# The sum of the state-space group's small products in the pool of the coefficients instead of that of the activations' parts

## The chip, the cores and the metric

The kernel runs on one core of a Trainium2 chip. The metric is the device time of one execution in microseconds (us), as the median of several runs. A profiled execution is one more run, from which the trace comes.

The core's engines work side by side and each takes its instructions in a fixed order: TensorE (PE) multiplies, VectorE (DVE), ScalarE (ACT) and GpSimd (POOL) work on elements, and SyncE (SP) issues the transfers from and to memory. An instruction that has to wait holds up all that stands behind it on its engine. On SP it is a transfer's issue that waits, and what stands behind it is the next transfers.

## The reference

Two layers, each of three sublayers. In between lies the mixing sublayer, one group of which is a diagonal complex state-space model (S5).

```python
h = layer_norm(ALPHA*h + 0.5*swiglu(h, ffn1_in[l], ffn1_out[l]), ...)    # "f1"
h = layer_norm(ALPHA*h + concat(pool, nsa, s5)(h @ w_in) @ w_out, ...)   # "mix"
h = layer_norm(ALPHA*h + 0.5*swiglu(h, ffn2_in[l], ffn2_out[l]), ...)    # "f2"

def swiglu(x, w_in, w_out):
    gate, up = split(x @ w_in, 2);  return (silu(gate) * up) @ w_out

def s5_mixer(u, ...):        # 16 groups, 64 complex states each
    ar, ai = exp(lr*dt) * (cos(li*dt), sin(li*dt))
    bbr, bbi = (fr, fi) * (b_re, b_im)               # complex product
    h = associative_scan(h[t] = a*h[t-1] + bb @ u[t])
    y = Re(c @ h) + d_skip*u;   ...
```

Sizes: 512 tokens, width 1024, 2816 hidden columns in the feed-forward parts, all in fp32.

## The kernel before

**Products.** Every fp32 operand of a large product is split into two parts, a rounded one (`hi`, made by ACT) and the rest (`lo`, made by DVE), and the product is three matmuls: hi·hi, hi·lo, lo·hi. Weights come in units of 128x1024. SP loads a unit into one of three buffers `st` (line 97), ACT and DVE split it (lines 131 and 132) into a slot of `ring`, or into the pair `wh`/`wl`, six places in all. A place comes free when PE has used the unit that lies there, and an `st` buffer when the unit in it has been split.

**The first feed-forward part of a layer, `ffn` with kind f1.** The hidden columns come in 22 tiles of 128. Tiles 0 to 3 and 18 to 21 are made by `pair` (lines 343 to 345 on PE, two PSUM banks `g` and `u`, then ACT's silu at line 547 and DVE's product at line 548), the rest by `quad`. Then `project` multiplies by the output weights: for each tile k, 24 matmuls (line 491) into eight PSUM banks `o`, which are all the banks there are. Before tile k its activations are split into `ap`k by `split` (lines 602 and 603), one tile ahead. The eight banks `o` rotate with all other PSUM tiles: a bank is taken over once its last reader is done.

**The state-space matrices, `s5_matrices`.** It is a generator that `ffn` steps: one step before the pairs 18 to 21, six after pair 20, and one at each of the first tiles of `project` (`STEPS_AT`, `GB_AT`). POOL computes the complex products (`cmul`, lines 759 to 764): the matrices `ebr`, `ebi`, the coefficients `fcr`, `fci`, `nfci` in the tile `s5cf`, the matrices `gr`, `gi`, and by doubling the tables `tabc`, `tabs` with the scratch tile `dbl`. PE makes sixteen small products of these into the bank `kk` (lines 796 and 798), DVE adds the input's `dm` and writes the sum to `s5kk` (line 803), and eight small transfers carry blocks of `s5kk` to their places in `tm` (line 816).

**Two pools.** `pp` ("parts") has four buffers of 4 KB in each partition, used in turn by whoever asks next: `s5raw`, `s5d`, `s5ebr`, `s5ebi`, `s5kk`, and after these the parts `ap0`, `ap1`, ... Whoever takes a buffer waits until all readers of its last holder are done. The second pool ("s5t", `ap2` in `s5_matrices`) has two buffers, for `s5cf` and `dbl`. When `s5_matrices` is through, that pool is closed, and the memory goes to `ln_g` and `ln_b`, the norm's scale and shift, whose loads (lines 424 and 425) therefore wait for the end of all work on the tiles of "s5t".

The program's order on each engine is worked out when the kernel is built, before it runs; an instruction's place in it depends on when its buffers and inputs were reckoned to be free.

Of the kernel before, what the change touches and what calls it, by code (L numbers as in the profile page):

```python
# [216 lines left out]
class Trunk:  # L217
# [526 lines left out]
    def s5_matrices(self, l, ap, ap2):  # L744
# [10 lines left out]
        def slot(name, pool=ap):  # L755
            return pool.tile([128, 8, 128], F32, tag="u", name=name)
# [37 lines left out]
        for j in range(8):  # L794
# [4 lines left out]
                             start=False, stop=True)  # L799
            if j % 2 and j < 7:  # L800
                yield
        kks = slot("s5kk").rearrange("p a b -> p (a b)")[:, :256]
        ve.tensor_tensor(kks, kk[:, :256], dm, op=ALU.add)
        yield
        for src, dst in ((ebr, self.er), (ebi, self.ei)):
# [870 lines left out]
```

## Time and profile before

| | |
|---|---|
| Median of 3 runs | 1946.25 us (1940.8, 1946.25, 1946.46) |
| Profiled execution, its own time | 1939.41 us |
| Its span, first to last instruction | 1937.6 us |
| Mean granted clock of TensorE | 0.987 of full speed |
| PE busy | 1875.5 us (97%) |
| DVE busy | 1365.1 us (70%) |
| ACT busy | 811.3 us (42%) |
| POOL busy | 528.1 us (27%) |

The time of the profiled execution is 1.81 us above its span; the median of the three runs lies 6.84 us above the profiled execution. PE is busy nearly all the time, so a stretch in which it is not is looked up by itself, with what ended it.

### The profile page before, as it was taken

To read this page: it belongs to the slowest core of one execution; us is meant where nothing else is said; L and a number is where in the kernel's file an instruction comes from. 1 tells how busy PE (TensorE), PEld (TensorE's weight loads), DVE (VectorE), ACT (ScalarE), POOL (GpSimd) and SP (SyncE) were. 2 spreads that over 40 slices of the span, in tenths; PEclk is the share of its full clock that TensorE was granted. 3 is DMA by queue.
4 is the path that set the end of the run, shared out by engine and by line. 5 is a ranking of instruction groups with operands and counts; after the bars stand their busy time and mean duration, and the time that the engine had idled before them with its cause. 6 is when DMAs were issued, how large, how long until landed. Compare 5 with 4: busy or idle time off the path is not lost.

```text
span 1937.6 us, 30490 instructions
## 1 busy us (share of the span) xinstructions
PE 1875.5 (97%) x12164; PEld 1672.8 (86%) x12164; DVE 1365.1 (70%) x1926; ACT 811.3 (42%) x1388; POOL 528.1 (27%) x539
## 2 busy tenths in 40 slices
PE   9999959999999999999999999699999999999998
PEld 7999848888788999998899997588887889999886
DVE  8998324667986889874598982246679768989634
ACT  5454213234772354543235442231457714455430
POOL 3332920104331433300043329101043313322001
PEclk9999979999999999999999999799999999999999
DMA  7233233222103132343203341341221122232421
GB/s 249 92 120 122 85 101 125 69 69 88 45 20 102 65 109 100 119 163 126 81 30 102 110 146 54 112 142 42 80 77 45 42 90 66 99 112 96 157 94 44
DMA packets 57214, 183.59 MB, mean 95 GB/s; under 512 B 11248, under 2 KB 12016, under 8 KB 57072
## 3 DMA queue, kind: packets, MB, share of 16 engines
q1 hardware_dynamic: 57072, 181.64, 28.3%
q8 instruction: 96, 1.57, 0.3%
q14 instruction: 46, 0.38, 0.1%
HBM read 179.19 MB, written 2.10 MB: 94 GB/s over the span
## 4 chain that ended last, share of the span: by engine, by line
PE 82%; POOL 7%; DVE 7%; DMA 2%; issue 1%; ACT 1%; SPq 1%; DVEq 0%; ACTq 0%; POOLq 0%
PE o L491 28%; PE qb L345 3%; PE qb L344 3%; PE qb L343 3%; PE qa L345 3%; PE qa L344 3%; PE qa L343 3%; PE qc L345 3%; PE qc L344 3%; PE qc L343 3%; PE o L1314 2%; PE pt L1298 2%; PE qd L345 2%; PE qd L344 1%; PE qd L343 1%; DVE ring L132 1%
## 5 line engine op out<-in xcount | busy, mean ns | idle before, releaser
L132 DVE TENSOR_TENSOR ring<-st,ring 128x1024 fp32r<-128x1024 f32 (+1 forms) x257 | 354.3, 1387 | 251.0 <-ACT ring L131 248.5
L131 ACT ACTIVATE ring<-st 128x1024 fp32r<-128x1024 f32 (+1 forms) x257 | 270.3, 1054 | 374.1 <-PE o L491 170.8
L491 PE MATMUL o<-ring,ap 128*128 128x512 f32 x1440 | 332.5, 392 | 43.9 <-DVE a L548 43.9
L491 PEld LDWEIGHTS o<-ring,ap 128*128 128x128 f32 x1440 | 272.3, 189 | 101.6 <-DVE a L548 44.7
L383 POOL TENSOR_TENSOR mv<-mv,expo 128x1 f32<-128x1 f32 x24 | 35.6, 1481 | 629.4 <-DVE mv L382 629.4
L182 POOL TENSOR_TENSOR st<-st,sb 128x512 f32<-128x512 f32 x64 | 95.5, 1493 | 186.4 <-DVE ring L132 114.3
L343 PE MATMUL qb<-th,ring 128*128 128x256 f32 x512 | 143.4, 280 | 0.4 <-DVE u L707 0.4
L343 PE MATMUL qa<-xh,ring 128*128 128x256 f32 x512 | 143.4, 280 | 0.0
L345 PE MATMUL qa<-xh,ring 128*128 128x256 f32 x512 | 143.4, 280 | 0.0
L344 PE MATMUL qa<-xl,ring 128*128 128x256 f32 x512 | 143.4, 280 | 0.0
L344 PE MATMUL qb<-tl,ring 128*128 128x256 f32 x512 | 143.4, 280 | 0.0
L345 PE MATMUL qb<-th,ring 128*128 128x256 f32 x512 | 143.4, 280 | 0.0
L491 PE MATMUL o<-wh,ap 128*128 128x512 f32 x448 | 125.5, 391 | 0.0
L177 POOL TENSOR_TENSOR sumg<-sb 128x512 f32<-128x512 f32 x32 | 57.4, 1792 | 177.8 <-DMA sb<-in_ffn_in 177.8
L132 DVE TENSOR_TENSOR wl<-st,wh 128x1024 fp32r<-128x1024 f32 x51 | 62.2, 1228 | 56.3 <-ACT wh L131 56.0
L491 PEld LDWEIGHTS o<-wh,ap 128*128 128x128 f32 x448 | 83.5, 188 | 17.6 <-DVE vw L717 0.6
L344 PEld LDWEIGHTS qa<-xl,ring 128*128 128x128 f32 x512 | 97.6, 191 | 0.1
L344 PEld LDWEIGHTS qb<-tl,ring 128*128 128x128 f32 x512 | 97.6, 191 | 0.0
L343 PEld LDWEIGHTS qb<-th,ring 128*128 128x128 f32 x512 | 96.4, 188 | 0.5 <-issue 0.5
L343 PEld LDWEIGHTS qa<-xh,ring 128*128 128x128 f32 x512 | 96.3, 188 | 0.2
L345 PEld LDWEIGHTS qa<-xh,ring 128*128 128x128 f32 x512 | 96.1, 188 | 0.0
L345 PEld LDWEIGHTS qb<-th,ring 128*128 128x128 f32 x512 | 96.1, 188 | 0.0
(459 smaller groups left out, 5159.5 us busy)
## 6 DMA issues: line engine op xcount, KB each, us to landing
st<-in_ffn_in SPq DMA_DIRECT2D x110, 512.0 KB, 3.3
st<-in_ffn_out SPq DMA_DIRECT2D x88, 512.0 KB, 3.3
sb<-in_ffn_in SPq DMA_DIRECT2D x64, 512.0 KB, 3.3
st<-in_w_out SPq DMA_DIRECT2D x16, 512.0 KB, 3.8
st<-in_w_b SPq DMA_DIRECT2D x8, 512.0 KB, 4.4
st<-in_w_a SPq DMA_DIRECT2D x8, 512.0 KB, 4.6
ln_g<-in_ln_g SPq DMA_DIRECT2D x6, 512.0 KB, 4.1
ln_b<-in_ln_b SPq DMA_DIRECT2D x6, 512.0 KB, 5.5
```

Of the source, the lines that this page charges most:

```text
L131: self.nc.scalar.activation(hi, t, AF.Copy)
L132: self.nc.vector.tensor_tensor(lo, t, hi.bitcast(F32), op=ALU.subtract)
L177: po.tensor_tensor(s[:, f], b[:, f], b[:, r], op=ALU.add)
L182: po.tensor_tensor(a[:, f], a[:, f], b[:, f], op=ALU.subtract)
L343: mm(out, lhsT=ah, rhs=bh, start=start, stop=False, skip_group_check=skip)
L344: mm(out, lhsT=ah, rhs=bl, start=False, stop=False, skip_group_check=skip)
L345: mm(out, lhsT=al, rhs=bh, start=False, stop=stop, skip_group_check=skip)
L383: nc.gpsimd.tensor_tensor(mv[:, 2:3], mv[:, 2:3], self.expo, op=ALU.pow)
L491: mm(ps[t][f], lhsT=a[:, q], rhs=w[:, 512 * f:512 * f + 512], start=(k == first and a is ah and w is wh), stop=end)
L1298: nc.tensor.transpose(ps[:, 128 * k:128 * k + 128], p[:, i, 128 * k:128 * k + 128], ident)
L1314: mm(o[64 * i:64 * i + 64], lhsT=self.v[:, b, k, 64 * g:64 * g + 64], rhs=pt[:, i, 128 * k:128 * k + 128], start=False, stop=b == 1 and k ...
```

## The change

The tile `s5kk` is taken from the pool "s5t" instead of "parts". One call differs:

```diff
@@ -799,7 +799,7 @@ def s5_matrices(self, l, ap, ap2)
                              start=False, stop=True)
             if j % 2 and j < 7:
                 yield
-        kks = slot("s5kk").rearrange("p a b -> p (a b)")[:, :256]
+        kks = slot("s5kk", ap2).rearrange("p a b -> p (a b)")[:, :256]
         ve.tensor_tensor(kks, kk[:, :256], dm, op=ALU.add)
         yield
```

No instruction is added, none is taken away, and none has another size. What changes is who takes which buffer after whom. In "parts", `ap0` now takes the buffer of `s5raw` (before: of `s5d`), `ap1` that of `s5d` (of `s5ebr`), `ap2` that of `s5ebr` (of `s5ebi`), `ap3` that of `s5ebi` (of `s5kk`), and `ap4` follows `ap0` (before `ap0` too, from its other place). In "s5t", `s5cf` has the first buffer as before, `s5kk` has the second, and `dbl` takes the first after `s5cf` (before: the second, which was empty). The order on PE is the same; on the other engines it moves at the following places, here in layer 0, and at the same ones in layer 1.

ACT, where the product with the output weights begins: `ei` is the last copy of the state-space matrices, `ap_2462`, `ap_2465`, `ap_2523` and `ap_2599` are `ap0` to `ap3`, `wh_2492` is unit 4 of the output weights and `ring<-st_2418` unit 5, and `a_2340<-g_2390` is the silu of tile 21.

```order
 L810 ACTIVATE ei<-et_2380 128x512
-L602 ACTIVATE ap_2462<-a_242 128x512
 L602 ACTIVATE ap_2465<-a_242 128x512
 L602 ACTIVATE ap_2523<-a_396 128x512
+L602 ACTIVATE ap_2599<-a_396 128x512
 L131 ACTIVATE wh_2492<-st_2338 128x1024
 L547 ACTIVATE a_2340<-g_2390 128x512
-L602 ACTIVATE ap_2599<-a_396 128x512
 L131 ACTIVATE ring<-st_2418 128x1024
```

The split of `ap3` moves ahead of unit 4 and of the silu; on DVE its second half moves in the same way, from a place ahead of the product of tile 21 (line 548) to one behind the halves of `ap1` and `ap2`.

ACT, some 13 instructions earlier: `a_2217<-g_2159` is the silu of tile 18, `wh_2246` and `ring<-st_2187` are the two weight units of tile 21, and `ring<-st_2215` is unit 0 of the output weights.

```order
 L547 ACTIVATE a_2217<-g_2159 128x512
 L131 ACTIVATE wh_2246<-st_2088 128x1024
+L602 ACTIVATE ap_2462<-a_242 128x512
 L131 ACTIVATE ring<-st_2187 128x1024
 L131 ACTIVATE ring<-st_2215 128x1024
```

The split of `ap0` has come here; it takes the buffer of `s5raw`, so it waits for POOL's last product that reads `s5raw`.

SP, the transfers around the norm's loads: `st_2418`, `st_2446`, `st_2496` and `st_2552` are the units 5, 6, 7 and 8 of the output weights. First where `ln_g` stood, then where it stands.

```order
 L97 DMA st_2418<-in_ffn_out 128x1024
-L424 DMA ln_g<-in_ln_g 128x1024
-L816 DMA tm<-s5kk 16x8x16
-L816 DMA tm<-s5kk 32x8x16
-L816 DMA tm<-s5kk 48x8x16
-L816 DMA tm<-s5kk 64x8x16
 L97 DMA st_2446<-in_ffn_out 128x1024
```

```order
+L816 DMA tm<-s5kk 64x8x16
+L424 DMA ln_g<-in_ln_g 128x1024
 L97 DMA st_2496<-in_ffn_out 128x1024
+L425 DMA ln_b<-in_ln_b 128x1024
 L97 DMA st_2552<-in_ffn_out 128x1024
```

Before, `ln_g` stood ahead of all eight transfers to `tm` and of unit 6; now it stands behind them, and ahead of unit 7.

POOL, the end of `gr` and `gi` and the beginning of the doubling.

```order
+L763 TENSOR_TENSOR s5cf<-s5cf,prm_a4r 128x256
+L764 TENSOR_TENSOR gi<-gi,s5cf 128x16x16
+L822 TENSOR_SCALAR gi<-gi 128x1024
+L760 TENSOR_TENSOR dbl<-tabs 128x8
+L761 TENSOR_TENSOR tabc<-tabc,dbl 128x8
+L763 TENSOR_TENSOR dbl<-tabs,tabc 128x8
+L759 TENSOR_TENSOR tabc<-tabc 128x8x2
```

Before, the instructions of the first four doublings stood between those of `fcr`, `gr` and `gi`; now all that write `dbl` stand behind the last of `gi`.

## Rows read from the trace of the kernel before

**Rows 1.** The page: the chain that ended last, by engine.

```profile
PE 82%; POOL 7%; DVE 7%; DMA 2%; issue 1%; ACT 1%; SPq 1%; DVEq 0%; ACTq 0%; POOLq 0%
```

**Rows 2.** Waits from 236 to 268 us: who waited for whom, total, times, longest.

```profile
ACT ap L602 <- DMA tm<-s5kk: 28.3, 1, 28.3
...
PE o L491 <- DVE a L548: 22.0, 1, 22.0
```

**Rows 3.** Timeline of PE, both layers: start, length, line, operands, count [idle before].

```profile
227.13 1.52 PE L809 MATMUL et<-cst,s5ebi 128*128 128x128 f32 x8
...
239.41 4.47 PE L491 MATMUL o<-ring,ap 128*128 128x512 f32 x19
...
265.83 19.27 PE L491 MATMUL o<-ring,ap 128*128 128x512 f32 x77 [21.95 <-DVE a L548]
284.94 0.62 PE L491 MATMUL o<-wh,ap 128*128 128x512 f32 x2
...
1202.14 4.47 PE L491 MATMUL o<-ring,ap 128*128 128x512 f32 x19
...
1247.57 0.62 PE L491 MATMUL o<-wh,ap 128*128 128x512 f32 x2
```

**Rows 4.** Stretches: width, busy PE, PEld, DVE, ACT, POOL, granted clock, DMA, GB/s.

```profile
266.00:268.00 2.00, 2.00 (x5) 1.61 (x6) 0.91 (x1) 0.00 (x0) 0.00 (x0) 0.50 0.66 229
268.00:270.00 2.00, 2.00 (x8) 1.53 (x8) 0.49 (x1) 1.58 (x2) 0.00 (x0) 0.73 0.71 248
```

**Rows 5.** The chain in order of time, two links: start, length.

```profile
254.16 1.27 POOL tabs L764
...
265.18 0.61 DVE a L548
```

**Rows 6.** SP: the issue of `ln_g` and the next, and its longest wait.

```profile
255.45 0.33 SPq L424 DMA_DIRECT2D ln_g<-in_ln_g  x1
255.83 2.75 SPq L816 DMA_DIRECT2D tm<-s5kk  x4
...
SPq L424 <- POOL tabs L764: 29.8, 1, 29.8
```

**Rows 7.** Timeline of POOL, layer 0, and its last doubling in layer 1.

```profile
206.64 1.60 POOL L762 TENSOR_TENSOR s5cf<-s5raw,prm_fi 128x256 f32<-128x256 f32 x1
...
214.60 0.61 POOL L763 TENSOR_TENSOR s5cf<-s5raw,prm_fr 128x256 f32<-128x256 f32 x1
...
230.72 1.06 POOL L763 TENSOR_TENSOR s5cf<-s5cf,prm_a3r 128x256 f32<-128x256 f32 x1
...
1217.15 1.26 POOL L764 TENSOR_TENSOR tabs<-tabs,dbl 128x512 f32<-128x512 f32 x1
```

**Rows 8.** Timeline of DVE: two beside POOL's products, two in a step of `project`.

```profile
206.36 1.41 DVE L132 TENSOR_TENSOR ring<-st,ring 128x1024 fp32r<-128x1024 f32 x1 [3.97 <-ACT ring L131]
...
229.87 2.46 DVE L603 TENSOR_TENSOR ap<-a,ap 128x512 fp32r<-128x512 f32 x3 [3.77 <-ACT ap L602]
...
275.35 1.23 DVE L132 TENSOR_TENSOR ring<-st,ring 128x1024 fp32r<-128x1024 f32 x1 [4.01 <-ACT ring L131]
276.50 0.69 DVE L603 TENSOR_TENSOR ap<-aq,ap 128x512 fp32r<-128x512 f32 x1
```

**Rows 9.** Timeline of ACT: unit 7 and `ap5`, then unit 8, in `project`.

```profile
274.26 1.06 ACT L131 ACTIVATE ring<-st 128x1024 fp32r<-128x1024 f32 x1 [4.26 <-PE o L491]
275.23 0.61 ACT L602 ACTIVATE ap<-aq 128x512 fp32r<-128x512 f32 x1
279.70 1.06 ACT L131 ACTIVATE ring<-st 128x1024 fp32r<-128x1024 f32 x1 [3.86 <-PE o L491]
```

**Rows 10.** Transfers of a unit, us to landing: 258 to 259.2, 262.6 to 263, all.

```profile
st<-in_ffn_out SPq DMA_DIRECT2D x1, 512.0 KB, 4.4
...
st<-in_ffn_out SPq DMA_DIRECT2D x1, 512.0 KB, 5.4
...
st<-in_ffn_out SPq DMA_DIRECT2D x88, 512.0 KB, 3.3
```

## The prediction

> **What bounds the kernel now.** I read the page first, then the waits of a stretch, then the timelines of each engine in it. The chain that ended last runs over PE for 82% of the span, so time is to be had only where PE stands still or where the chain leaves it. It leaves it for POOL for 7% of 1937.6 us, some 135 us [rows 1]. In the chain in order of time this is two runs of the state-space matrices, one in each layer, of which the first ends at 255.43 us with the last doubling and then, through SP, a transfer to `tm` and ACT, comes to DVE's line 548 and so back to PE [rows 5]. The list of waits tells the same from the other end: ACT waits 28.3 us ahead of a split (line 602) for the transfer to `tm`, and PE 22.0 us for line 548 [rows 2].
>
> With the order of the program the links can be named. SP's queue holds `ln_g` ahead of the eight small transfers to `tm`. `ln_g` waits 29.8 us, until the last doubling is done, since it takes over the memory of the coefficients' pool [rows 6]. The transfers to `tm` are held up behind it, though their input was ready long before. `ap3` takes the buffer of `s5kk`, which these transfers read, so ACT stands at `ap3` until they have landed. On DVE the product of tile 21 (line 548) is queued behind `ap3`'s second half; it reads the last PSUM bank that `project` needs, so PE stops after 19 of the 24 matmuls of tile 0 [rows 3].
>
> **What a stop costs.** A step of `project` is 5.44 us (279.70 less 274.26 [rows 9]). Undisturbed, tile 4, the first with weights in `wh`, would begin 4 x 5.44 = 21.76 us after tile 0: at 261.17 and 1223.90 us. It begins at 284.94 and 1247.57 [rows 3]. That is 23.77 and 23.67 us late, 47.44 together. Of each, 21.95 us is the idle stretch; the rest fits the granted clock afterwards, 0.50 (1.2 GHz) from 266 to 268 us and 0.73 in the mean up to 270 [rows 4]: (1 - 0.50) x 2 + (1 - 0.73) x 2 = 1.5 us, and 0.1 before 266.
>
> **What the change does to this.** No instruction comes or goes, so nothing is paid for work. `ap3` takes the buffer of `s5ebi`, free once PE has transposed it at about 228.7 us [rows 3], and stands before the silu of tile 21 on ACT. The wait for `tm` is gone, and with it the 47.44 us. Three waits are new or moved.
>
> *First, ap0 waits for `s5raw`* and stands on ACT early, in the pairs of tiles 18 to 21. POOL's last product that reads `s5raw` ended at 215.21 us [rows 7]. ACT will stand there until then, and behind it are two weight splits (1.0 us each), the silu of tile 19 (as long as `ap`'s first half, 0.6 [rows 9]) and more; DVE stands too, at `ap0`'s second half. The first that PE misses is the bank which the silu of tile 19 empties: the last of the four groups of transposes takes it, half way through the row at 227.13, near 227.9 us [rows 3]. So `ap0` may start as late as 227.9 - 0.6 - 2.0 - 0.6 = 224.7 us. It has 9.5 us to spare, more if POOL is quicker while DVE stands. The weights behind it are wanted later still, at the second half of tile 21. I cost this at nothing; from below because a split that PE doesn't yet want can give nothing, from above by those 9.5 us.
>
> *Second, the doublings* of 1 to 8 columns now run in a row behind `gi` rather than among other products. POOL's work stays the same, but its end may move. Two things move it. (a) POOL is slowed beside DVE: the product at 206.64 took 1.60 us beside DVE's weight split, against 0.61 for one of the same size at 214.60, and one beside `ap`'s second halves took 1.06 [rows 7, 8]. So a weight split costs POOL 1.0 us and a second half of `ap` 0.45. Until 256 us DVE will now do, beyond what it did before, the splits of units 5 and 6 and the second halves of `ap3` and `ap4`: 2 x 1.0 + 2 x 0.45 = 2.9 us. (b) Each of some 24 doubling products now waits for the one before it, where they were interleaved. I take 0.04 us each, 1.0 us; between 0 and 0.13 each the bounds are 0 and 3 us. In all 3.9 us, between 0 and 5.9.
>
> For (a) there is a rule too. The Trainium skill, page "SBUF — State Buffer", section "Who interferes with whom", says that a VectorE `tensor_tensor` with two inputs in SBUF contends with a GpSimd instruction that reads SBUF, and that the one that comes later is blocked for the whole instruction. By that rule, with DVE's lengths of 1.23 and 0.69 us [rows 8], (a) would be 2 x 1.23 + 2 x 0.69 = 3.8 us rather than 2.9. The trace agrees in kind: 0.99 us were added beside a split of 1.41.
>
> *Third, `ln_g` still waits for the doublings,* and unit 7 of the output weights is now queued behind it on SP; on ACT the split of unit 7 stands ahead of that of `ap5` [rows 9], so PE's tile 5 hangs on it. Counted from the start of `project`: the last doubling ended after 16.0 us in layer 0 (255.43 - 239.41) and 16.3 us in layer 1 [rows 3, 5, 7]; with 3.9 more after 20.1. `ln_g` is issued, and 0.4 us later [rows 6] unit 7. A unit lands after 3.3 us as a rule, after 4.4 behind `ln_g` and some of `tm`, after 5.4 behind `ln_b` [rows 10]. I take 4.4, the row behind `ln_g`: unit 7 is there after 24.9 us. Tile 5 begins after 5 x 5.44 = 27.2 us, and wants `ap5`'s first half then, which is ready 0.97 + 0.61 = 1.6 us after unit 7; and the second half 4 matmuls or 0.9 us later, which is ready 2.9 us after unit 7 (277.19 less 274.26 [rows 8, 9]). So unit 7 must be there after 25.2 us. It is, by 0.3 us. With both upper bounds (16.3 + 5.9 + 0.4 + 5.4 = 28.0) PE would wait 2.8 us in each layer, with the lower ones not at all. Since 0.3 us is less than what I don't know, I take 0.5 us in each layer. In the kernel before the same queue cost nothing, because PE stood still anyway.
>
> The rest of SP's queue is no danger: the transfers to `tm` no longer stand behind `ln_g`, so they go out as soon as `s5kk` is written, up to the 29.8 us of that wait [rows 6] earlier.
>
> **The sum.** 47.4 - 2 x 0.5 = 46.4 us less. Against the profiled execution's own time, 1939.41: 1893.0 us. The median of the three runs lies 6.84 us above it; two of three runs were there, one and the profiled one were not, so I add half, 3.4, and predict **1896 us** (2.6% below the median of before). What is gained in `project` isn't given back: behind it PE is the chain again.
>
> **Rivals.**
> *A. A new stop at tile 5.* The mechanism of the third point, with a doubling run or a landing beyond my bounds. For it: the margin is 0.3 us, and DVE, so far at rest during POOL's last 16 us, now works. Against it: ACT and DVE stand at unit 7 by then, so DVE stops slowing POOL. If unit 7 lands 5 us late, 10 us of 47 are lost, and the time is 1896 + 9 = 1905 us. By the page's rule alone unit 7 lands 0.9 us later, 0.6 past its limit, which is inside what I took.
> *B. Slower: ACT's wait at `ap0`.* Its place is the first point. It costs from 224.7 us on, one for one, and decides the sign from 224.7 + 23.7 = 248.4 us: POOL would have to leave `s5raw` 33 us later than it did. At 40 us later in each layer, the time is 1946 + 2 x 7 = 1960 us. Nothing in the trace holds POOL that long; its wait for the load of `s5raw` stands before all this and isn't touched.
> *C. No change:* the stop has a second cause that ends at the same moment, as units not loaded or a bank not free. Against it: the wait's only releaser is `tm` [rows 2], and what ACT had behind `ap3` ran at once. The time would be 1946 us.
>
> **Chances.** The forecast 0.80, A 0.13, B 0.04, C 0.03. A measurement of this kernel can tell about 0.3% from no change, 5.8 us, which is also the spread of the three runs. Faster is the forecast and A, 0.93; same 0.03, slower 0.04. The range: at its lower end no new stop and a median as low as the profiled execution, 1892, less 2 for the runs' spread; at its upper end the stop of 2.8 us in each layer, 1892.0 + 5.6, and the whole 6.8: 1904, and 2 for the lesser half of A. So 1890 to 1906.
>
> **What would show it.** Right: no row of PE waiting for line 548 near 244 us in either layer; tile 4 some 21.8 us after tile 0; POOL's part of the chain near nothing; ACT waiting at line 602 for POOL up to about 215 us; the last doubling near 259 us and unit 7 landed near 264. Wrong: a wait of PE ahead of tile 5, near 266.6 us, with ACT behind unit 7's transfer, by more than 3 us (A); PE waiting near 228 us for a bank (B); the same stop with another releaser (C).

## The result and the profile after

The changed kernel takes 1898.17 us (median of 4 runs, 1896.81 to 1901.27), the kernel before 1946.36 us on the same chip (4 runs, 1940.8 to 1949.62). The ratio is 0.9758, with a 95% interval of 0.9732 to 0.9783: 48.2 us less by the medians. The forecast was 1896 us, within 1890 to 1906. The profiled execution of the changed kernel took 1899.04 us, with a span of 1897.1 us and a mean granted clock of 0.997; before these were 1939.41, 1937.6 and 0.987. One execution, the profiled one of e8 below, took 3090.99 us at a mean granted clock of 0.556 and stays out of every comparison.

The page of the changed kernel: busy time by engine, PE and its granted clock in 40 slices, and the chain that ended last.

```profile
PE 1875.3 (99%) x12164; PEld 1672.4 (88%) x12164; DVE 1372.8 (72%) x1926; ACT 810.6 (43%) x1388; POOL 527.4 (28%) x539
...
PE   9999999999999999999999999999999999999998
...
PEclk9999999999999999999999999999999999999999
...
PE 81%; POOL 8%; DVE 7%; DMA 2%; issue 1%; ACT 1%; SPq 0%; DVEq 0%; ACTq 0%; POOLq 0%
```

PE's busy time is what it was, 1875.3 us against 1875.5; the span shrank by 40.5 us, so what went is idle time. But POOL still has 8% of the chain, after 7% before [rows 1]. This is the first sign that something new stops PE behind POOL. The timeline of PE shows it, in `project` of layer 0 and then of layer 1.

```profile
240.16 21.92 PE L491 MATMUL o<-ring,ap 128*128 128x512 f32 x96
261.92 0.61 PE L491 MATMUL o<-wh,ap 128*128 128x512 f32 x2
...
269.69 29.33 PE L491 MATMUL o<-ring,ap 128*128 128x512 f32 x120 [2.17 <-ACT ap L602]
...
1183.36 21.92 PE L491 MATMUL o<-ring,ap 128*128 128x512 f32 x96
...
1211.83 1.19 PE L491 MATMUL o<-ring,ap 128*128 128x512 f32 x4 [1.10 <-ACT ap L602]
1213.17 26.59 PE L491 MATMUL o<-ring,ap 128*128 128x512 f32 x116 [0.15 <-DVE ap L603]
```

The first four tiles run through, 96 matmuls in a row, where before 19 were followed by a stop of 21.95 us [rows 3]. Tile 4 begins 21.76 us after tile 0 in both layers (1205.12 less 1183.36 in the second). Ahead of tile 5 there is a new, short stop: 2.17 us in layer 0, 1.10 and 0.15 in layer 1. The chain in order of time says what it hangs on.

```profile
260.64 1.30 POOL tabs L764
262.37 5.59 DMA st<-in_ffn_out
268.06 1.06 ACT ring L131
269.69 1.30 PE o L491 x4
```

POOL's last doubling ends, unit 7 is transferred, ACT splits it and then `ap5`, and PE goes on. SP's queue shows why a doubling holds up a weight unit.

```profile
228.17 5.39 SPq L816 DMA_DIRECT2D tm<-s5kk  x8
261.96 0.35 SPq L424 DMA_DIRECT2D ln_g<-in_ln_g  x1
262.37 0.42 SPq L97 DMA_DIRECT2D st<-in_ffn_out  x1
262.83 0.42 SPq L425 DMA_DIRECT2D ln_b<-in_ln_b  x1
```

All eight transfers to `tm` are issued from 228.17 us on, where the first began at 255.83 before [rows 6]. `ln_g` waits for the end of the doublings as it did, and unit 7 is now the transfer behind it. In the waits of all engines from 190 to 280 us (total, times, longest) this and the moved split `ap0` appear as follows.

```profile
ACT ring L131 <- DMA st<-in_ffn_out: 24.7, 3, 20.6
...
ACT ap L602 <- POOL s5cf L763: 14.5, 1, 14.5
...
PE o L491 <- ACT ap L602: 2.2, 1, 2.2
```

ACT's wait for `tm` and PE's 22.0 us for line 548 [rows 2] are gone. ACT stands 14.5 us at `ap0` and 20.6 us at unit 7; PE feels nothing of the first, and 2.2 us of the second.

### The profile page after: what moved, and what is told of

The parts are those of the page before. It is cut to its first block, busy times and chain, and to the rows that moved or that the text cites. A ratio compares the mean times of both kernels' runs of the same rounds, so it can differ in the third digit from the quotient of the medians.

```text
span 1897.1 us, 30481 instructions
## 1 busy us (share of the span) xinstructions
PE 1875.3 (99%) x12164; PEld 1672.4 (88%) x12164; DVE 1372.8 (72%) x1926; ACT 810.6 (43%) x1388; POOL 527.4 (28%) x539
## 4 chain that ended last, share of the span: by engine, by line
PE 81%; POOL 8%; DVE 7%; DMA 2%; issue 1%; ACT 1%; SPq 0%; DVEq 0%; ACTq 0%; POOLq 0%
PE o L491 26%; PE qb L345 3%; PE qb L343 3%; PE qb L344 3%; PE qa L345 3%; PE qa L343 3%; PE qa L344 3%; PE qc L345 3%; PE qc L343 3%; PE qc L344 3%; PE o L1314 2%; PE pt L1298 2%; PE qd L345 2%; PE qd L343 2%; PE qd L344 2%; DVE ring L132 1%
## 5 line engine op out<-in xcount | busy, mean ns | idle before, releaser
L132 DVE TENSOR_TENSOR ring<-st,ring 128x1024 fp32r<-128x1024 f32 (+1 forms) x257 | 358.3, 1402 | 255.3 <-ACT ring L131 252.9
L177 POOL TENSOR_TENSOR sumg<-sb 128x512 f32<-128x512 f32 x32 | 51.0, 1595 | 178.0 <-DMA sb<-in_ffn_in 178.0
L491 PEld LDWEIGHTS o<-wh,ap 128*128 128x128 f32 x448 | 83.5, 188 | 17.6 <-DVE vw L717 0.6
```

Of the source, the lines that this page charges most:

```text
L132: self.nc.vector.tensor_tensor(lo, t, hi.bitcast(F32), op=ALU.subtract)
L177: po.tensor_tensor(s[:, f], b[:, f], b[:, r], op=ALU.add)
L491: mm(ps[t][f], lhsT=a[:, q], rhs=w[:, 512 * f:512 * f + 512], start=(k == first and a is ah and w is wh), stop=end)
```

## The experiments

Two theories say what the 47 us before hung on. **Q**, the queue: `ln_g`, waiting on SP for the doublings, stands ahead of the transfers to `tm`; whatever puts it behind them takes the stop away. **B**, the buffers: `ap3` takes over `s5kk`, so the cure is that `ap3` gets another buffer. The change does both at once. What is left after it, the stop at tile 5, was to be traced to the same queue, and the two parts of POOL's longer run, (a) DVE beside it and (b) the doublings in one row, to be told apart.

### e1: the changed kernel again

No edit; it is the measure for e2 to e4, with which it shared a chip.

> The changed kernel itself once more, as the thing that the other runs of this series stand beside on the same chip. 1898 us, within 3 us; PE stops ahead of tile 5 of the output product for 2.2 us in layer 0 and 1.3 us in layer 1.

1900.38 us (4 runs), before 1943.87 us (9 runs), ratio 0.9772 [0.9757, 0.9788]. The timeline of PE in this kernel, tile 5 in layers 0 and 1:

```profile
268.18 27.93 PE L491 MATMUL o<-ring,ap 128*128 128x512 f32 x120 [2.19 <-ACT ap L602]
...
1209.85 29.08 PE L491 MATMUL o<-ring,ap 128*128 128x512 f32 x120 [2.50 <-ACT ap L602]
```

The new stop is there again, 2.19 and 2.50 us, so it is no accident of one execution. Its length changes from one to the next, though, and in a third trace of the same program (e7 below) layer 1 has no stop at all.

### e2: the old buffers, with the norm's loads held back

The kernel before, in which `ln_g` and `ln_b` are each first written by a one-column copy that needs `ap12`. Their loads then come late in the program, and on SP behind `tm` and the units. `ap3` still takes the buffer of `s5kk`.

```diff
-                self.load_gb(*(gp.tile([128, D], F32, name=n) for n in ("ln_g", "ln_b")), l, ln_i)
+                ts = [gp.tile([128, D], F32, name=n) for n in ("ln_g", "ln_b")]
+                if f1:
+                    for t in ts:
+                        nc.scalar.activation(t[:, :1], parts[GB_AT][0][:, :1].bitcast(F32), AF.Copy)
+                self.load_gb(*ts, l, ln_i)
```

> The kernel before, with s5kk left in the pool of the parts, but with the loads of the norm's scale and shift made to depend on ap12, by a copy of one column (two ACT instructions in each layer), so that they stand late in SP's queue, behind unit 16 of the output weights. Theory Q (the gain came from SP's queue: what held ap3 was that the small transfers stood behind ln_g): the whole 47.4 us are gone, and the stop at tile 5 isn't there either, so 1895 us, 3 below the changed kernel. Theory B (the gain came from the buffers: ap3 has to give up the buffer of s5kk, since its transfers land late in any case): PE still stops after 19 matmuls, and the time stays within 10 us of 1946.

1893.91 us (4 runs), ratio 0.9739 [0.9724, 0.9755]. The timeline of PE in `project` of layer 0:

```profile
239.53 21.92 PE L491 MATMUL o<-ring,ap 128*128 128x512 f32 x96
...
266.73 27.36 PE L491 MATMUL o<-ring,ap 128*128 128x512 f32 x120
```

and of SP's queue:

```profile
227.54 5.40 SPq L820 DMA_DIRECT2D tm<-s5kk  x8
...
290.59 0.33 SPq L424 DMA_DIRECT2D ln_g<-in_ln_g  x1
```

Neither stop is there. With `ln_g` out of the way the transfers to `tm` go out from 227.54 us on, and `ap3` has its buffer in time although it is still that of `s5kk`, in the kernel as built. The buffer does no harm by itself: what Q says of this run holds, and what B says of it (a stop after 19 matmuls, a time near 1946 us) does not. The page of this kernel shows how little of the chain POOL still has:

```profile
PE 90%; DVE 7%; issue 1%; DMA 1%; ACT 1%; POOL 1%; SPq 0%; DVEq 0%; ACTq 0%
```

POOL is down to 1% of the chain, which I had expected of the change itself.

### e3: the changed kernel, with the norm's loads held back

The same edit in the changed kernel.

> The changed kernel with the same late loads of scale and shift. If the stop at tile 5 (2.2 and 1.3 us) comes from unit 7 standing behind ln_g, it goes, and the time is 3.4 us below the changed kernel of this series, 1895 us. If it came from ACT or DVE being late after their wait at ap0, it stays, and the time is that of the changed kernel. Beside the kernel before with late loads it tells what the move of s5kk is worth once the queue is right: nothing, within 2 us, by theory Q; some 45 us by theory B.

1893.21 us (5 runs), ratio 0.9735 [0.9721, 0.9749]. Its timeline of PE has no stop, and in the waits from 195 to 300 us `ap0` stands:

```profile
ACT ap L606 <- POOL s5cf L767: 14.7, 1, 14.7
```

Two things follow. First, e3 and e2 are equal (0.7 us apart, within what the runs of one kernel scatter): once the queue is in order, it is worth nothing that `s5kk` lies in the other pool. ACT's early wait of 14.7 us at `ap0`, which e3 has and e2 has not (its other buffers keep it away), costs nothing either, as the prediction's first point said. Second, e3 is 7.2 us faster than e1. In e1's trace the two stops sum to 4.69 us, and the 120 matmuls behind them took 0.57 and 1.72 us longer than the 27.36 us of e2: 7.0 us. So the rest of what `ln_g` costs in the changed kernel is accounted for by the stop ahead of tile 5 and the matmuls just behind it, as closely as runs that scatter by 4 us can tell.

### e4: a tile of its own for the sum

The changed kernel, with `s5kk` in a pool of its own (1 KB in each partition). It takes nobody's buffer, and nobody takes its own while it matters. `dbl` then has an empty buffer, as before the change, the doublings stand among the other products again, and `ln_g` again ahead of `tm` and of unit 6.

```diff
-                steps = self.s5_matrices(l, pp, right(gbc, "s5t", 2))
+                t2 = right(gbc, "s5t", 2)
+                self.kks = right(gbc, "s5k", 1).tile([128, 256], F32, name="s5kk")
+                steps = self.s5_matrices(l, pp, t2)
...
-        kks = slot("s5kk", ap2).rearrange("p a b -> p (a b)")[:, :256]
+        kks = self.kks
```

> s5kk in a tile of 1 KB of its own, in neither pool, so that ap3 takes the buffer of s5ebi as in the changed kernel, but the doubling can start early as in the kernel before, and ln_g is again put ahead of the small transfers and of unit 6 in SP's queue. Theory Q: the old stop is gone since ap3 hangs on no transfer, but unit 6 now lands some 27 us after the start of the output product (last doubling at 19, four small transfers 3, landing 4.4 to 5.4), and ap4, behind it on ACT, is wanted at 21.8: a new stop of about 7 us ahead of tile 4 in each layer and a slow clock behind it, 1905 to 1912 us. Theory B: the buffers are right, so it is as fast as the changed kernel or 3 us faster, 1895 to 1898.

1907.18 us (4 runs), ratio 0.981 [0.9796, 0.9825]: 6.8 us slower than e1. The timeline of PE:

```profile
270.20 1.04 PE L491 MATMUL o<-wh,ap 128*128 128x512 f32 x2 [4.79 <-ACT ap L604]
...
1215.94 1.22 PE L491 MATMUL o<-wh,ap 128*128 128x512 f32 x2 [5.09 <-ACT ap L604]
```

and of SP's queue in layer 0:

```profile
261.06 0.33 SPq L424 DMA_DIRECT2D ln_g<-in_ln_g  x1
261.44 2.76 SPq L818 DMA_DIRECT2D tm<-s5kk  x4
264.30 0.57 SPq L97 DMA_DIRECT2D st<-in_ffn_out  x1
```

No buffer is short, the old stop is gone, and yet PE stops 4.8 and 5.1 us, one tile earlier than in e1: unit 6 stands behind `ln_g` and four transfers to `tm`. That is Q again, by another route. Which unit stands behind `ln_g` sets which tile waits. The time is in the range that I gave for Q; the stops are shorter than the 7 us that I expected, since unit 6 landed some 25 us after the start of `project` and not 27. With the matmuls of tile 4 behind them, which took 7.2 and 7.1 us instead of 5.44, the stops make 13.3 us, and e4 is 14.0 us slower than e3, which has none.

The run says something of B as well. `ln_g` stands ahead of the transfers to `tm` here as it did before the change, and a buffer other than that of `s5kk` for `ap3` is enough to take the old stop away: 36.7 us less than the kernel before. The old stop thus needed both, the place of `ln_g` and `ap3`'s buffer. B is wrong in that the buffer is not needed for the gain (e2) and does not bring all of it (e4), where the place of `ln_g` does.

### e5: the last doubling twice

The changed kernel, with the last doubling done twice, to see whether a longer run of POOL goes into the stop one for one.

```diff
+            for _ in range(1 + (2 * n == NCH)):
                 cmul(tc[:, :, hi], ts[:, :, hi], tc[:, :, lo], ts[:, :, lo], cn, sn, tmp[:, :, :n])
```

> The changed kernel with the last doubling of the tables done twice (same values), six products of POOL more, 6.9 us in each layer. In SP's order ln_g now stands behind unit 7 and ahead of unit 8. If the stop is set by the end of the doubling through SP's queue, it moves to tile 6 and grows: last doubling some 28.5 us after the start of the output product, unit 8 landed at 35, wanted at 6 x 5.44 + 0.9 - 2.9 = 30.6, so some 4.5 to 5.5 us in each layer instead of 2.2 and 1.3, and the time is 6 to 9 us over the changed kernel, 1904 to 1907 us. If the stop has nothing to do with POOL's end, it stays at tile 5 with its length, or is gone, and the time is 1895 to 1898.

1908.47 us (4 runs, 1905.3 to 1911.74), before 1942.29 us (13 runs), ratio 0.9827 [0.981, 0.9843]. The timeline of PE in layers 0 and 1:

```profile
279.45 24.06 PE L491 MATMUL o<-ring,ap 128*128 128x512 f32 x96 [3.29 <-ACT ap L602]
...
1226.38 23.59 PE L491 MATMUL o<-ring,ap 128*128 128x512 f32 x96 [6.58 <-ACT ap L602]
```

In layer 0 the stop is 3.29 us. In both it has moved on by one tile: 96 matmuls are left behind it up to the next tile with weights in `wh`, not 120, so it stands ahead of tile 6. The longer run is paid for: 9.9 us of stops, against 3.4 in the changed kernel's own trace, where I expected 9 to 11. They are not alike in the two layers because POOL's run began 48.8 us before `project` in layer 0 and 46.0 us before it in layer 1, so the doublings ended 27.3 and 30.5 us after its start, where I took 28.5 for both. The 96 matmuls behind the stops took 2.1 and 1.7 us longer than the 21.92 us of the undisturbed ones, of which the expectation says nothing; the time is 1.5 us above the upper end that I gave.

### e6 and e7: an empty tile that takes a buffer

Each takes one tile from a pool and never touches it, to shift who follows whom: e6 in the kernel before, in the pool of the coefficients, to bring the doublings behind `gi`; e7 in the changed kernel, in the pool of the parts, to give `ap0` its old predecessor.

```diff
# e6
+        slot("fill", ap2)
         kks = slot("s5kk").rearrange("p a b -> p (a b)")[:, :256]
# e7
+        slot("fill")
         kks = slot("s5kk", ap2).rearrange("p a b -> p (a b)")[:, :256]
```

> The kernel before with an empty tile taken from the coefficients' pool, so that dbl follows s5cf there as in the changed kernel, and s5kk stays in the parts' pool: half of the change alone, the half that makes POOL's end later. SP's order is that of before. By the theory that the stop runs from the last doubling one for one, it gets longer by what the later doubling costs without DVE's extra work, (b) of the prediction, 1.0 us (0 to 3), plus the clock: 2 us over the kernel before, 0 to 6. If moving the doubling costs POOL much more than that, as waits of each product for the last, it is over 10 us slower.

> The changed kernel with an empty tile taken from the parts' pool where s5kk was, meant to bring back the rotation of before in that pool (ap0 after s5d, ap3 after the empty tile). In the order that comes out ap0 still stands early on ACT and waits for the buffers, so it tells whether the new early wait of ap0 depends on which buffer it gets. By the prediction's first point that wait costs nothing: the time is that of the changed kernel, 1898 us within 3, and ACT still stands ahead of ap0 for some 14 us.

Neither did what it was meant to. e6: 1941.49 us (10 runs), ratio 0.9994 [0.9983, 1.0004]; the first product into `dbl` is still at 211.23 us, among the others, and SP's order is that of before. e7: 1899.17 us (4 runs), ratio 0.9777 [0.9761, 0.9793], and `ap0` still waits for POOL, 14.4 us. A tile that nothing uses gets no buffer: as built, e6 is the kernel before and e7 the changed kernel, instruction for instruction. The pool hands out what is free, and does not deal strictly in turn as I had described it: in the kernel before, `ap0` lies where `s5ebr` lay and `ap1` where `s5d` lay; after the change `ap1` follows `s5ebr` and `ap2` follows `s5d`. For `ap3`, on which the argument rests, the description holds. As tests of a theory both runs are void; as repeats they serve. The timelines of PE, first the old stops of e6 in its two layers, then the matmuls from tile 5 on in layer 1 of e7:

```profile
265.45 19.17 PE L491 MATMUL o<-ring,ap 128*128 128x512 f32 x77 [23.27 <-DVE a L548]
...
1227.62 19.35 PE L491 MATMUL o<-ring,ap 128*128 128x512 f32 x77 [21.90 <-DVE a L548]
...
1216.24 27.36 PE L491 MATMUL o<-ring,ap 128*128 128x512 f32 x120
```

The old stop of layer 0 is 23.27 us here against 21.95 in the first trace. POOL's run began 46.6 us before `project` in this execution and 47.8 in the first, and was 0.4 us longer, so the doublings ended 17.6 us after the start of `project` and not 16.0. When POOL's run begins, measured against PE, differs from one execution to the next. In layer 1 of e7 it began early and was short, and PE goes on to tile 5 without a stop.

### e8 and e9: the doublings behind gi in the old order

The kernel before, with a filler that is really used: written before `kk` is summed, and last by a copy of one column of `gi` when that is done. `dbl` can only follow it, so the doublings stand in one row, while SP and ACT keep the old order. This does part (b) of the change alone, with two tiny instructions more.

```diff
+        fill = slot("fill", ap2)
+        po.memset(fill[:, 0, :1], 0.0)
         kks = slot("s5kk").rearrange("p a b -> p (a b)")[:, :256]
...
         po.tensor_scalar(self.gi, self.gi, -1.0, None, op0=ALU.mult)
+        po.tensor_copy(fill[:, 0, :1], self.gi[:, 0, :1])
```

> The kernel before, with a filler tile in the coefficients' pool that is held until gi is done (written by one small POOL memset at the place of s5kk, and once more by a one-column POOL copy behind gi), so that dbl must take the buffer of s5cf: now the order on POOL does have all of the doubling behind gi, and SP's and ACT's order are those of before. From the lost overlap seen between the kernels with late loads, POOL's run should get 2.2 us longer with no more work of DVE beside it, and the old stop with it, one for one: 24 us instead of 22 in each layer, 4 to 5 us over the kernel before, 0.2%. If the stop in the kernel before doesn't hang on POOL's end, nothing changes, within 2 us.

> The same kernel once more for an undisturbed trace. POOL's run from the first product to the last doubling: before 63.8 and 62.8 us; here 66.0 and 65.0 if the 2.2 us of lost overlap are all that moving the doubling costs. PE's stop after 19 matmuls: 24 us in each layer instead of 22.

e8 gave 1947.4 us (11 runs) against 1943.94 (16 runs of before), ratio 1.0017 [1.0006, 1.0028]: 3.3 us slower, between 1.2 and 5.4, where I expected 4 to 5. The trace is that of e9, the same kernel (1947.2 us in one run, and one of before 1948.35). The timeline of PE in e9:

```profile
270.42 19.37 PE L491 MATMUL o<-ring,ap 128*128 128x512 f32 x77 [25.68 <-DVE a L548]
...
1235.90 19.60 PE L491 MATMUL o<-ring,ap 128*128 128x512 f32 x77 [24.74 <-DVE a L548]
```

POOL's run, from the start of its first product (line 759 on `s5raw`) to the end of its last doubling, is 66.84 and 65.39 us in the two layers, 3.05 and 2.57 more than before (63.79 and 62.82), and the stop is 3.7 and 2.8 us longer, where I expected 2. That it follows POOL's end one for one is seen over all six old stops that have a trace (before, e6, e9): each is 5.7 to 6.1 us longer than the time from the start of `project` to the end of the doublings, which went from 16.0 to 19.6 us. How much of the longer run is (b) comes below.

## Why the prediction was right, point by point

**The old stop.** It was to cost 47.44 us and to go. It went, wholly: e3, which has no stop in either place, is 50.7 us faster than before, e2 50.0. Profiled execution against profiled execution (1939.41 us before, 1893.95 and 1891.64) it is 45.5 and 47.8, so the 47.44 fits what it was taken from. That the 2.5 to 3.2 us more by the medians are only the old stop's own variation (1.3 us in e6) was not shown; it stays open. The mechanism was named rightly: the chain from the doublings over `ln_g`, `tm` and `ap3` to line 548 was what stopped PE. What I had not seen is what its links are worth. It can be broken at `ln_g`'s place on SP alone (e2), and then everything is gained, or at `ap3`'s buffer alone (e4), and then 36.7 us are, because `ln_g` goes on holding up a unit of weights. The change breaks both; with `ln_g` out of the way the buffer adds nothing (e2 against e3).

**First, ap0.** Right: ACT's wait lasted 14.5 us, and its row in the timeline of ACT is

```profile
213.60 0.63 ACT L602 ACTIVATE ap<-a 128x512 fp32r<-128x512 f32 x1 [14.46 <-POOL s5cf L763]
```

The split began 11 us before the limit of 224.7 that I had worked out. PE has no wait there. Rival B, the slower one, had nothing to stand on.

**Second, POOL's run.** I took 3.9 us more, with 5.9 as the upper bound. It became 4.6 us longer in layer 0 (68.40: 193.53 to 261.93) and 5.8 in layer 1 (68.66: 1136.02 to 1204.68). Split by its 97 instructions, the sums of their durations and what their rows overlap:

| us, layer 0 / layer 1 | sum of durations | overlap | run |
|---|---|---|---|
| before | 66.81 / 65.65 | 3.02 / 2.83 | 63.79 / 62.82 |
| after | 69.14 / 69.34 | 0.74 / 0.68 | 68.40 / 68.66 |
| e2, old order of POOL | 71.57 / 73.30 | 2.91 / 2.96 | 68.66 / 70.34 |
| e3, new order of POOL | 70.80 / 72.18 | 0.67 / 0.79 | 70.13 / 71.39 |
| e9, new order of POOL | 67.56 / 66.00 | 0.72 / 0.61 | 66.84 / 65.39 |

(a), the durations, grew by 2.3 and 3.7 us where I took 2.9; with e1 and e7 six layers are on record, 1.7 to 3.7 us and 2.7 in the mean: right. The first of the two splits that I counted is this one, in the timelines of DVE and POOL:

```profile
241.28 1.23 DVE L132 TENSOR_TENSOR ring<-st,ring 128x1024 fp32r<-128x1024 f32 x1 [0.16 <-ACT ring L131]
...
241.15 0.22 POOL L763 TENSOR_TENSOR dbl<-tabs,tabc 128x8 f32<-128x8 f32 x1
241.32 1.25 POOL L759 TENSOR_TENSOR tabc<-tabc 128x16 f32<-128x16 f32 x1
...
243.69 0.24 POOL L759 TENSOR_TENSOR tabc<-tabc 128x32 f32<-128x32 f32 x1
```

The product at 241.32 took 1.25 us beside DVE's split of 241.28 to 242.51, and one of twice its size 0.24 a little later: 1.0 us was added. The product began 0.04 us behind DVE's split and ended 0.06 us behind it. The Trainium skill, page "SBUF — State Buffer", section "SBUF: two separate sides", says that of two such instructions the one that starts first has the shared ports for its whole length, and the other is blocked. The trace agrees here. By that rule (a) would have been 3.8 us. My rows gave 2.9, and the mean of the six layers, 2.7, is nearer to them.

(b), the lost overlap, is 2.2 us and not 1.0: this term was mis-sized. The table shows it in each pair that differs in POOL's order alone or nearly so: e2 to e3 2.2 us in both layers, before to e9 2.3 and 2.2. When products that don't need each other alternate, the next row begins some 0.04 us before the last one ends; where a product needs the one just ahead it begins about 0.08 us after it (240.85 less 240.77). In layer 0, 8 of the 96 steps from one row to the next were of this second kind before the change, and 27 are after it: 19 x 0.12 = 2.3 us. Only 7 of the 19 lie in the doublings behind `gi`. The other 12 lie among the products of `gr` and `gi`, which the doublings no longer separate. I had looked at the doublings alone, counted 24, and taken 0.04 us each, a price for which I had no row.

**Third, unit 7.** Here the step failed that read "so unit 7 must be there after 25.2 us. It is, by 0.3 us". The limit fits the runs, the time of the unit did not. Three traces of this program show six cases, in us from the start of `project`:

| | doublings' end | unit 7 landed | stop ahead of tile 5 |
|---|---|---|---|
| forecast | 20.1 | 24.9 | 0.5 |
| after, layers 0 and 1 | 21.8 / 21.3 | 27.8 / 26.7 | 2.17 / 1.25 |
| e1 | 21.7 / 22.6 | 27.8 / 28.1 | 2.19 / 2.50 |
| e7 | 21.6 / 19.0 | 27.9 / 24.3 | 2.25 / none |

PE stops in the five cases in which the unit lands after 25.2 us and not in the sixth. Three terms were off. (b) is the first. The second is one that I had put at nothing: POOL's run begins 44.9 to 47.7 us before `project` in these six, while the 16.0 and 16.3 us that I started from hold the 47.8 and 46.6 of one trace; layer 0 of the first execution lost over 1 us by this. The third is the landing: I took 4.4 us, the row behind `ln_g` and parts of `tm`. The issues' time to landing, unit 7 in layers 0 and 1:

```profile
st<-in_ffn_out SPq DMA_DIRECT2D x1, 512.0 KB, 5.6
...
st<-in_ffn_out SPq DMA_DIRECT2D x1, 512.0 KB, 5.0
```

It was nearest to the 5.4 of [rows 10], a unit issued directly behind another transfer of 512 KB, which is what unit 7 now is. I had kept that as the upper bound only. So the stop was 2.17 and 1.25 us where I took 0.5 each, inside the bound of 2.8: rival A's mechanism, at a size between the forecast and A. A margin of 0.3 us could not carry a forecast where the start of POOL's run alone moves by almost 3. And for a short stop I had allowed no slow clock. Behind the stop of layer 0 the windows of the changed kernel (width, PE, PEld, DVE, ACT, POOL, granted clock, DMA, GB/s) show it:

```profile
269.60:271.60 2.00, 1.87 (x5) 1.17 (x6) 1.40 (x3) 1.15 (x3) 0.00 (x0) 0.76 0.55 217
271.60:273.60 2.00, 2.00 (x6) 1.59 (x5) 2.00 (x3) 1.93 (x3) 0.00 (x0) 0.50 0.72 260
```

The 120 matmuls took 29.33 us instead of the 27.36 of e2, so 2.0 us went there, and 0.4 in layer 1. With 3.4 us of stops the third point cost 5.8 us, not 1.0.

**The sum.** By its own base, the profiled execution, I forecast 1893.0; the one after took 1899.04, 6.0 more, of which this third point explains 4.8; the rest is within what the executions of one kernel scatter. The median came within 2.2 us of the forecast with the help of the 3.4 us that I added for the distance between profile and median: before, the median lay some 7 us above the profiled execution, after, 0.9 below it. Part of the closeness is thus luck: two errors against each other. Rival C fell with the old stop.

**What would show it.** Three of the marks were right as written: no wait for line 548, tile 4 after 21.8 us, ACT at line 602 for POOL. The doublings' end (261.9, not 259) and the landing (268.0, not 264) were late. "POOL's part of the chain near nothing" was wrong, 8%: with a stop of 2 us at its end the chain still leaves PE for POOL's whole run. Its share tells where the chain goes, not what can be gained there: removing it (e3) gave 7.2 us, not 150.

## What to carry to other kernels

When one pool's memory goes to a load, look at what is queued behind that load on the issuing engine: it waited 30 us for its memory, and it was its place, not the wait, that cost. An edit of a few lines that moves it behind the units that are wanted early gave all that the change gave and 6.5 and 7.2 us more, in the two arrangements of the buffers. When a margin comes out at a fraction of a us, price the landing by the row with the same neighbour ahead, and each stop of PE with the clock behind it, and take from more than one execution when an engine off the chain begins its run.

## What the runs showed of the chip that I had not expected

A stop of PE of about 2.2 us cost almost as much again in slow clock in one case and no slow clock in another. In the changed kernel the granted clock fell to 0.50 (1.2 GHz) behind the stop of 2.17 us, and so it did in e7 behind that of 2.25 us. In e1, behind that of 2.19 us in layer 0, it stayed at 1.00 (2.4 GHz), and behind that of 2.50 us in layer 1 it fell. The windows of e1:

```profile
268.00:270.00 2.00, 1.67 (x6) 1.11 (x7) 1.47 (x2) 1.15 (x3) 0.00 (x0) 1.00 0.60 242
...
1209.80:1212.00 2.20, 2.15 (x5) 1.77 (x6) 1.43 (x3) 1.19 (x2) 0.00 (x0) 0.53 0.81 296
```

So the cost of a short stop can't be read from its length alone; what decides between the two was not tried.

The order of POOL's instructions changes its time apart from any contention: by the starts and ends of their rows, the same 97 instructions take 2.2 us longer (e2 against e3) when products that need each other stand one behind the other than when they alternate with others.
